# Six column tiles of the gated convolution computed as block products, and the skip term of the scan on ScalarE

## The chip, the cores and the metric

One NeuronCore of one Trainium2 chip runs the whole layer as a single program. The metric is device time in microseconds (us) of one execution. Executions of the kernel before took 2042.07, 2046.02 and 2046.38 us, median 2046.02 us.

## The reference

One layer of a hybrid decoder, 1024 positions by 1024 channels, all in float32. After a modulated RMS norm, one input projection makes five things: `z`, the `x/B/C` of a Mamba-2 scan, `dt`, the three inputs of a gated convolution, and two gates. What the change touches is this part:

```python
y_ssd = ssd_branch(z, xbc, dt_raw, ...)          # conv4 + silu, chunked scan, gate silu(z), grouped norm
#   in ssd_branch, after the scan:
y = y + d_skip[:, None] * xh                     # the skip term
y = y * silu(z); y = grouped_rmsnorm(y, norm_g, 4)
y_sc  = sc_b * causal_dwconv(sc_c * sc_h, conv_w)   # the gated convolution, 3 taps
mix   = (g_ssd * (y_ssd @ w_ssd_out) + g_sc * (y_sc @ w_sc_out)) @ w_o
```

The scan runs over 4 groups of 8 heads and, within a group, over 8 chunks of 128 positions with a state carried from chunk to chunk. The gated convolution has 1024 channels, so its three inputs are 24 column tiles of 128 channels. After the mixer comes a second half (norm, a gated MLP with convolution) that the change leaves alone.

## The kernel before, in words

Every float32 matrix is split into a rounded high part and a rest (line 130 on ScalarE, line 131 on VectorE), and a product is the sum of three products of such parts. A column tile of 128 channels by 1024 positions costs 48 matmuls of 128x512 this way (`gemm_into`, lines 147 to 156).

**Pair stage.** `Pair` (lines 178 to 276) computes two column tiles at once as a 2x2 block product with seven block multiplications instead of eight (the Strassen-Winograd scheme): 7 times 12 matmuls, 84 in place of 96. A loop over the string on line 621 computes 8 pairs of z, 8 pairs of gates and 12 pairs of x/B/C this way. Results go to DRAM.

**Scan.** Then come 32 chunks (`chunks`, line 807). Each chunk `n` is in three pieces: `ssd_front` loads `xb` and `zt` (for two chunks at once) and `E` (the cumulated decay, read with one row spread over all partitions), transposes `xb` (`xT`) and makes `xdt`, `sm`, `Bt`; `ssd_decay` makes on ScalarE `Cs` (an exponential), eight Relu operations on `E` and one exponential of it, and on VectorE the products with `xb` (line 717) and `sm` (line 727); `ssd_back` runs 16 pairs of small matmuls (`y`, line 737) that need `E`, `Cs` and the state of the chunk before, the matmul `st` of the new state, the norm of the two chunks before (matmuls into `half`), the skip term (line 765, four operations on VectorE that read `xb` and the finished `y`), the gate `zt` (line 767) and the square for the norm (line 769). `E`, `xb`, `zt` and `yo` have two buffers each, `xw` one and `state` two.

Between the pieces the loop on lines 810 to 817 puts pieces of the gated convolution. `sc_tile(i)` computes the three column tiles of 128 channels (`scc`, `sch`, `scb`) with plain `gemm`, in six steps of 24 matmuls; `STEPS` says how many steps follow each front: 0 to 2, 10 in a group of 8 chunks, 40 in all. The last 8 steps run after the scan. In this document these 128x512 matmuls between the chunks are called the column matmuls, and the matmuls of a chunk that start with `y` name the chunk: `y0_4` is group 0, chunk 4.

**Order.** The program is not run in the order written. A scheduler in the building library fixes the order on each engine before the run; calls inside `kept(...)` keep their place. On the chip every engine takes its list in that order and waits where an operand is missing. DMAs are issued by SyncE (SP), also in a fixed order.

After the scan `branches` multiplies the results by the output weights; it reloads `y_d` into tiles of the pool `qp` (`y_r`, line 845) and splits them.

```python
STEPS = (0, 1, 1, 2, 1, 2, 1, 2)
...
    if n + 1 < len(chunks):
        front = ssd_front(*chunks[n + 1])
    for _ in range(STEPS[n % 8]):
        next(proj, None)
    ssd_back(*this)
    if n + 1 < len(chunks):
        decay = ssd_decay(front)
```

Of the kernel before, what the change touches and what calls it, by code (L numbers as in the profile page):

```python
# [33 lines left out]
def hybrid_kernel(ctx: ExitStack, tc: tile.TileContext, x, pack, row_p, ada_w, w_in,  # L34
                  w_ssd, w_sc, w_o, w_up, w_down, out):
    nc = tc.nc
    V, S, G, PE, SY = nc.vector, nc.scalar, nc.gpsimd, nc.tensor, nc.sync
# [44 lines left out]
    def kept(ins):  # L82
        return tc.keep_in_program_order(ins)
# [4 lines left out]
    cv = {}  # L88
# [17 lines left out]
    ysc_d = [dram.tile([P, T], F32, name=f"ysc_d{i}") for i in range(KT)]  # L106
# [340 lines left out]
    def operands():  # L447
        return {n: [] for n in ("11", "12", "22", "s1", "s2", "s3", "s4")}
# [41 lines left out]
    A1 = operands()  # L490
# [121 lines left out]
    def gate_pair(g, j):  # L612
        us = Pair(A1, w_in[65 + j], w_in[66 + j], f"g{j}").finish()
        for o in range(2):
            S.activation(us[o], us[o], AF.Tanh, scale=0.5)
            SY.dma_start(gate_d[j + o], us[o])

    zs = [(z_pair, g, j) for g in range(NG) for j in (0, 2)]
    xs = [(xbc_pair, g, j) for g in range(NG) for j in (0, 2, 4)]
    gs = [(gate_pair, 0, 2 * n) for n in range(8)]  # L620
    for kind in "zzggggggggxxzxzxxzxxzxxzxxzx":
        fn, g, j = dict(z=zs, x=xs, g=gs)[kind].pop(0)
        fn(g, j)
# [18 lines left out]
    ld = ph.pool("ld", 2)  # L642
    sw = ph.pool("sw", 1)
# [5 lines left out]
    def bc(ap, n):  # L649
        return ap.unsqueeze(2).to_broadcast([P, ap.shape[1], n])  # L650
# [6 lines left out]
    def ssd_norm():  # L657
# [52 lines left out]
    def ssd_decay(front):  # L710
        nm, g, c, xb, zt, cs, hs, E, xdt, sm, Bt = front
        tS = tokS[:, c]
        Cs = cd = xw = None
        if c > 0:
            Cs = sw.tile([P, 8, P], F32, tag="Cs", name=f"Cs{nm}", bufs=2)
            S.activation(Cs, E, AF.Exp)  # L716
            V.tensor_tensor(Cs, Cs, xb[:, 5, cs].unsqueeze(1).to_broadcast([P, 8, P]), op=ALU.mult)
        if c < NCH - 1 and c > 0:
            cd = small.tile([P, 8], F32, tag="cd", name=f"cd{nm}")
            S.activation(cd, E[:, :, P - 1], AF.Exp)  # L720
        if c < NCH - 1:
            xw = sw.tile([P, 8, 64], F32, tag="xw", name=f"xw{nm}")
            G.tensor_tensor(xw, xdt, bc(tS[:, 3, hs], 64), op=ALU.mult)  # L723
        for h in range(8):
            S.activation(E[:, h, :], E[:, h, :], AF.Relu, scale=-1.0, bias=tS[:, 0, g * 8 + h:g * 8 + h + 1])  # L725
        S.activation(E, E, AF.Exp, scale=-1.0)  # L726
        V.tensor_tensor(E, E, sm.unsqueeze(1).to_broadcast([P, 8, P]), op=ALU.mult)  # L727
        return Cs, cd, xw

    def ssd_back(front, decay):  # L730
        nm, g, c, xb, zt, cs, hs, E, xdt, sm, Bt = front
        Cs, cd, xw = decay
        state = pairs.get("state")
        pt = bank(f"y{nm}")
        for j in range(4):
            def ymm(o, lhs, rhs, first, last):
                return PE.matmul(pt[o * 64:o * 64 + 64, j * P:j * P + P], lhs[:, 2 * j + o, :], rhs[:, 2 * j + o, :],  # L737
                                 start=first, stop=last)
            for o in range(2):
                ins = ymm(o, xdt, E, True, c == 0)  # L740
            if c > 0:
                for o in range(2):
                    ins = ymm(o, state, Cs, False, True)
        kept(ins)
        if c < NCH - 1:
            pst = bank(f"st{nm}")
            PE.matmul(pst, Bt, xw.rearrange("p h d -> p (h d)"), start=True, stop=True)  # L747
            pst = pst.rearrange("p (h d) -> p h d", h=8)
            ns = sw.tile([P, 8, 64], F32, tag="state", name=f"state{nm}", bufs=2)
            if c > 0:  # L750
                G.tensor_tensor(ns, state, bc(cd, 64), op=ALU.mult)
                V.tensor_tensor(ns, pst, ns, op=ALU.add)
            else:
                S.copy(ns, pst)
            pairs["state"] = ns
        if late:
            ssd_late()
        if pend:
            ssd_norm()
        if c % 2 == 0:  # L760
            pairs["out"] = ld.tile([P, 4, 256], F32, tag="yo", name=f"yo{nm}")
        yo = pairs["out"]
        y2 = yo[:, :, cs]
        for i in range(4):
            V.scalar_tensor_tensor(yo[:, i, cs], xb[:, i, cs], cv["ssd_d"][:, g * 4 + i:g * 4 + i + 1],  # L765
                                   pt[:, i * P:(i + 1) * P], op0=ALU.mult, op1=ALU.add)
        V.tensor_tensor(y2, y2, zt[:, :, cs], op=ALU.mult)
        sq = scratch.rearrange("p (a b) -> p a b", a=4)
        S.activation(sq, y2, AF.Square, scale=512 ** -0.5)
# [6 lines left out]
    def sc_tile(i):  # L776
        W = load_split(w_in[41 + i * 3], f"wsc{i}")
        pc = yield from gemm(A1p, W, f"scc{i}")
        ct = evt(f"sct{i}")
        S.copy(ct, pc)  # L780
        yield
        W = load_split(w_in[41 + i * 3 + 1], f"wsh{i}")
        ph = yield from gemm(A1p, W, f"sch{i}")
        V.tensor_tensor(ct, ph, ct, op=ALU.mult)
        w = cv["sc_w"][:, i * 3:i * 3 + 3]
        u = evt(f"scu{i}")
        S.activation(u, ct, AF.Copy, scale=w[:, 2:3])
        for k in (1, 0):
            s = 2 - k
            V.scalar_tensor_tensor(u[:, s:], ct[:, :T - s], w[:, k:k + 1], u[:, s:], op0=ALU.mult, op1=ALU.add)  # L790
        yield
        W = load_split(w_in[41 + i * 3 + 2], f"wsb{i}")
        pb = yield from gemm(A1p, W, f"scb{i}")
        V.tensor_tensor(u, pb, u, op=ALU.mult)
        if i < KT - 1:
            SY.dma_start(ysc_d[i], u)
        else:
            tail.append(u)
        yield

    def projections():
        for i in range(8):
# [514 lines left out]
```

## Time and profile before

| | |
|---|---|
| Median of three runs | 2046.02 us |
| The profiled execution, its own time | 2045.67 us |
| Span of its trace | 2044.0 us |
| Pair stage, scan, last 8 steps | 78 to 615, 615 to 985, 985 to 1012 us of the span |
| Output products of the branches, rest | 1012 to 1330, 1330 to 2044 us |

Busy time of TensorE is a sum of records that overlap, since matmuls are pipelined: a matmul of 128x512 has a record of 0.39 us. "Idle before" is the time in which an engine had no record, and the name behind the arrow is what ended it. The median lies 0.35 us above the profiled execution.

### The profile page before, as it was taken

To read this page: it belongs to the slowest core of one execution; us is meant where nothing else is said; L and a number is where in the kernel's file an instruction comes from. 1 tells how busy PE (TensorE), PEld (TensorE's weight loads), DVE (VectorE), ACT (ScalarE), POOL (GpSimd) and SP (SyncE) were. 2 spreads that over 40 slices of the span, in tenths; PEclk is the share of its full clock that TensorE was granted. 3 is DMA by queue.
4 is the path that set the end of the run, shared out by engine and by line. 5 is a ranking of instruction groups with operands and counts; after the bars stand their busy time and mean duration, and the time that the engine had idled before them with its cause. 6 is when DMAs were issued, how large, how long until landed. Compare 5 with 4: busy or idle time off the path is not lost. (4 is left out here: it accounts for less than half of the span.)

```text
span 2044.0 us, 25283 instructions
## 1 busy us (share of the span) xinstructions
PE 1993.1 (98%) x9476; PEld 1599.2 (78%) x9476; DVE 1453.3 (71%) x2016; ACT 978.8 (48%) x1572; POOL 152.0 (7%) x183
## 2 busy tenths in 40 slices
PE   7999999999999999999999999999999999989997
PEld 3788888888887777777887878876888888868886
DVE  4966567767768787786766555378887777767876
ACT  4665455544547656554422442246554454544443
POOL 1200000000002222121000010021000000000002
PEclk9999999999999999999999999999999999999999
DMA  8233223233245556553686567252222222268362
GB/s 298 77 125 120 104 98 120 100 111 120 99 139 208 167 186 206 170 165 127 203 275 230 196 228 266 93 187 71 103 72 93 83 73 93 83 228 282 119 232 98
DMA packets 128426, 308.97 MB, mean 151 GB/s; under 512 B 11184, under 2 KB 40240, under 8 KB 128304
## 3 DMA queue, kind: packets, MB, share of 16 engines
q1 hardware_dynamic: 128304, 307.36, 43.9%
q8 instruction: 74, 1.21, 0.2%
q14 instruction: 48, 0.39, 0.1%
HBM read 241.65 MB, written 65.67 MB: 150 GB/s over the span
## 5 line engine op out<-in xcount | busy, mean ns | idle before, releaser
L1042 DVE SCALAR_TENSOR_TENSOR uv<-u_u,pk,uv 128x1023 f32<-128x1023 f32 (+1 forms) x88 | 107.2, 1279 | 7.4 <-ACT uv L1039 7.4
L130 ACT CAST u_t_hi<-u_t 128x512 fp32r<-128x512 f32 x88 | 54.7, 623 | 119.8 <-PE u_p L172 108.6
L130 ACT CAST wy_hi<-wy_raw 128x1024 fp32r<-128x1024 f32 x32 | 33.6, 1051 | 133.4 <-PE bps L858 83.4
L594 DVE SCALAR_TENSOR_TENSOR xv<-x_u,pk,xv 128x1023 f32<-128x1023 f32 (+2 forms) x72 | 87.1, 1279 | 4.9 <-ACT xv L591 4.9
L725 ACT ACTIVATE E<-E,tokS 128x128 f32<-128x128 f32 x256 | 80.5, 390 | 14.5 <-DMA E<-acs_d 13.8
L130 ACT CAST u_hi<-u_raw 128x512 fp32r<-128x512 f32 x66 | 41.0, 622 | 73.2 <-PE u_p L172 73.2
L131 DVE TENSOR_TENSOR u_t_lo<-u_t,u_t_hi 128x512 fp32r<-128x512 f32 x88 | 60.2, 687 | 21.2 <-ACT u_t_hi L130 21.1
L716 ACT ACTIVATE Cs<-E 128x1024 f32<-128x1024 f32 x28 | 29.7, 1060 | 75.3 <-DMA E<-acs_d 75.2
L131 DVE TENSOR_TENSOR wy_lo<-wy_raw,wy_hi 128x1024 fp32r<-128x1024 f32 x32 | 39.1, 1221 | 37.4 <-ACT wy_hi L130 37.4
L130 ACT CAST x_t_hi<-x_t 128x512 fp32r<-128x512 f32 x48 | 29.9, 624 | 59.2 <-PE x_p L172 33.8
L1039 ACT ACTIVATE uv<-u_u,pk 128x1024 f32<-128x1024 f32 x44 | 52.5, 1238 | 2.3 <-DVE u_u L260 1.7
L737 PE MATMUL y<-E,xdt 128*64 128x128 f32 x512 | 51.1, 279 | 1.6 <-issue 1.6
L1189 POOL TENSOR_TENSOR dss<-dss,dss 128x1 f32<-128x1 f32 x8 | 3.8, 478 | 623.4 <-PE dx L1117 600.0
L130 ACT CAST x_hi<-x_raw 128x512 fp32r<-128x512 f32 x36 | 22.4, 623 | 53.2 <-PE x_p L172 25.2
L131 DVE TENSOR_TENSOR x_t_lo<-x_t,x_t_hi 128x512 fp32r<-128x512 f32 x48 | 32.5, 687 | 21.1 <-ACT x_t_hi L130 21.1
L727 DVE TENSOR_TENSOR E<-E,sm 128x1024 f32<-128x1024 f32 x32 | 41.1, 1286 | 8.5 <-ACT E L726 8.3
L131 DVE TENSOR_TENSOR u_lo<-u_raw,u_hi 128x512 fp32r<-128x512 f32 x66 | 45.0, 684 | 2.6 <-ACT u_hi L130 2.5
L256 DVE TENSOR_TENSOR u_u<-u_p,u_q 128x512 f32<-128x512 f32 x22 | 15.2, 691 | 44.3 <-PE u_p L173 44.3
L723 POOL TENSOR_TENSOR xw<-xdt,tokS 128x512 f32<-128x512 f32 x28 | 32.4, 1157 | 187.6 <-PE st L747 158.8
L765 DVE SCALAR_TENSOR_TENSOR yo<-xb,pk,y 128x128 f32<-128x128 f32 x128 | 39.3, 341 | 7.1 <-PE y L737 6.8
L737 PE MATMUL y<-Cs,state 128*64 128x128 f32 x448 | 43.9, 273 | 0.0
L896 DVE SCALAR_TENSOR_TENSOR gt<-gt,bps 128x512 f32<-128x512 f32 x32 | 20.5, 683 | 32.5 <-PE bps L859 30.2
(1865 smaller groups left out, 6716.2 us busy)
## 6 DMA issues: line engine op xcount, KB each, us to landing
u_raw<-in_w_up_dram SPq DMA_DIRECT2D x44, 512.0 KB, 3.5
E<-acs_d SPq DMA_DIRECT2D x32, 512.0 KB, 4.7
wy_raw<-in_w_ssd_dram SPq DMA_DIRECT2D x32, 512.0 KB, 4.9
x_raw<-in_w_in_dram SPq DMA_DIRECT2D x24, 512.0 KB, 3.4
xbc_d<-xv SPq DMA_DIRECT2D x24, 512.0 KB, 2.8
xb<-xbc_d SPq DMA_DIRECT2D x16, 768.0 KB, 6.3
f_d<-uv SPq DMA_DIRECT2D x22, 512.0 KB, 2.6
dm<-f_d SPq DMA_DIRECT2D x44, 256.0 KB, 6.0
```

What stands on the lines that cost most here:

```text
L130: S.copy(hi, src)
L131: V.tensor_sub(lo, src, hi.bitcast(F32))
L594: V.scalar_tensor_tensor(v[:, s:], u[:, :T - s], w[:, k:k + 1], v[:, s:], op0=ALU.mult, op1=ALU.add)
L716: S.activation(Cs, E, AF.Exp)
L723: G.tensor_tensor(xw, xdt, bc(tS[:, 3, hs], 64), op=ALU.mult)
L725: S.activation(E[:, h, :], E[:, h, :], AF.Relu, scale=-1.0, bias=tS[:, 0, g * 8 + h:g * 8 + h + 1])
L727: V.tensor_tensor(E, E, sm.unsqueeze(1).to_broadcast([P, 8, P]), op=ALU.mult)
L737: return PE.matmul(pt[o * 64:o * 64 + 64, j * P:j * P + P], lhs[:, 2 * j + o, :], rhs[:, 2 * j + o, :], start=first, stop=last)
L765: V.scalar_tensor_tensor(yo[:, i, cs], xb[:, i, cs], cv["ssd_d"][:, g * 4 + i:g * 4 + i + 1], pt[:, i * P:(i + 1) * P], op0=ALU.mult, op1= ...
L896: V.scalar_tensor_tensor(gts[o], gts[o], 1.0, ps[:, o, :], op0=ALU.add, op1=ALU.mult)
L1039: S.activation(v, us[j], AF.Identity, scale=w[:, 2:3], bias=cv["ffn_b"][:, t:t + 1])
L1042: V.scalar_tensor_tensor(v[:, s:], us[j][:, :T - s], w[:, k:k + 1], v[:, s:], op0=ALU.mult, op1=ALU.add)
```

## The change

Three parts. (1) The first two of the eight `sc_tile`s (`SCP = 2`, six of the 24 column tiles) leave the scan and become three pairs in the pair stage: `sch` and `scc` of tile 0, the same of tile 1, then `scb` of tiles 0 and 1 together, which reads the convolved values back from DRAM. The string of the pair stage gets three letters `s`, among the gates. `STEPS` sinks to 7 in a group, 28 in all. (2) The skip term: ScalarE multiplies `xb` by `ssd_d` into `yo` in `ssd_decay` of every second chunk (four operations of 128x256), and VectorE adds the finished `y` in one operation of 128x512. (3) `yo` gets three buffers; `xw` and `state` move into the rotating pool `qp` of ten tiles.

```diff
+SCP = 2
+    def sc_pair(b, i):
+        if not b:
+            ct, u = Pair(A1, w_in[41 + i * 3], w_in[42 + i * 3], f"sch{i}").finish()
+            V.tensor_tensor(ct, ct, u, op=ALU.mult)
+            sc_taps(i, ct, u)
+            SY.dma_start(ysc_d[i], u)
+            return
+        us = Pair(A1, w_in[43 + i * 3], w_in[46 + i * 3], f"scb{i}").finish()
+        for o in range(2):
+            u = evt(f"scu{i + o}")
+            SY.dma_start(u, ysc_d[i + o])
+            V.tensor_tensor(us[o], us[o], u, op=ALU.mult)
+            SY.dma_start(ysc_d[i + o], us[o])
...
-    for kind in "zzggggggggxxzxzxxzxxzxxzxxzx":
+    for kind in "zzgggsggsggsgxxzxzxxzxxzxxzxxzx":
...
+        if c % 2 == 0:
+            yo = ld.tile([P, 4, 256], F32, tag="yo", name=f"yo{nm}", bufs=3)
+            for i in range(4):
+                S.activation(yo[:, i, :], xb[:, i, :], AF.Copy, scale=cv["ssd_d"][:, g * 4 + i:g * 4 + i + 1])
+            pairs["yo"] = yo
...
-            xw = sw.tile([P, 8, 64], F32, tag="xw", name=f"xw{nm}")
+            xw = qt(f"xw{nm}").rearrange("p (h d) -> p h d", h=8)
...
-            ns = sw.tile([P, 8, 64], F32, tag="state", name=f"state{nm}", bufs=2)
+            ns = qt(f"state{nm}").rearrange("p (h d) -> p h d", h=8)
...
-        for i in range(4):
-            V.scalar_tensor_tensor(yo[:, i, cs], xb[:, i, cs], cv["ssd_d"][:, g * 4 + i:g * 4 + i + 1],
-                                   pt[:, i * P:(i + 1) * P], op0=ALU.mult, op1=ALU.add)
+        V.tensor_tensor(y2, pt.rearrange("p (i l) -> p i l", i=4), y2, op=ALU.add)
...
-        for i in range(8):
+        for i in range(SCP, KT):
             yield from sc_tile(i)
...
-    STEPS = (0, 1, 1, 2, 1, 2, 1, 2)
+    STEPS = (0, 1, 1, 1, 1, 1, 1, 1)
```

The scheduler's order changes with it. On TensorE, in group 0, between the new state `st0_4` of chunk 4 and the `y` of chunk 5, before (12 column matmuls of `scb0` and `scc1` stand there):

```order
L747 MATMUL st0_4_5445<-xw0_4_5370,Bt0_4_5263 128x512
L670 MATMUL half_4958<-rs0_2_5355,ones_82 128x128
L695 MATMUL xT0_6_5491<-ident_77,xb0_6_5485 128x128 x4
L156 MATMUL scb0_5403<-h12_6h_681,wsb0_lo_5400 128x512
L156 MATMUL scb0_5403<-h22_6h_523,wsb0_lo_5400 128x512
L153 MATMUL scb0_5403<-h12_7h_699,wsb0_hi_5399 128x512
L154 MATMUL scb0_5403<-h12_7l_700,wsb0_hi_5399 128x512
L153 MATMUL scb0_5403<-h22_7h_542,wsb0_hi_5399 128x512
L660 MATMUL half_4958<-ones_82,scratch_170 128x1
```

The same place in the changed program, to the end of `y0_5`'s first pairs:

```order
L775 MATMUL st0_4_5850<-xw0_4_5777,Bt0_4_5697 128x512
L693 MATMUL half_5393<-rs0_2_5760,ones_82 128x128
L718 MATMUL xT0_6_5892<-ident_77,xb0_6_5886 128x128 x4
L683 MATMUL half_5393<-ones_82,scratch_170 128x1
L722 MATMUL half_5393<-xb0_6_5886 128x128
L724 MATMUL half_5393<-ident_77,xb0_6_5886 128x128
L765 MATMUL y0_5_5936<-E0_5_5789,xdt0_5_5796 64x128 x2
```

No column matmul stands between chunks 4 and 5 any more; 20 of `scb2` follow right behind `y0_5` instead. Between chunks 2 and 3 there are 5 (15 before), between 3 and 4 there are 4 (33 before).

On ScalarE, in group 0, the operations on chunk 5's `E` and what follows them in the changed program (`scratch` from `yo0_4` is the square of chunk 4; `yo0_6` are the new products with `ssd_d`):

```order
L744 ACTIVATE Cs0_5_5869<-E0_5_5789 128x1024
L748 ACTIVATE cd0_5_5872<-E0_5_5789 128x8
L753 ACTIVATE E0_5_5789<-E0_5_5789,tokS_180 128x128 x5
L730 COPY Bt0_5_5802<-half_5393 128x128
L753 ACTIVATE E0_5_5789<-E0_5_5789,tokS_180 128x128 x3
L740 ACTIVATE yo0_6_5973<-xb0_6_5886,pk_75 128x256
L754 ACTIVATE E0_5_5789<-E0_5_5789 128x1024
L740 ACTIVATE yo0_6_5973<-xb0_6_5886,pk_75 128x256 x3
L744 ACTIVATE Cs0_6_5978<-E0_6_5890 128x1024
L748 ACTIVATE cd0_6_5981<-E0_6_5890 128x8
L753 ACTIVATE E0_6_5890<-E0_6_5890,tokS_180 128x128
L792 ACTIVATE scratch_170<-yo0_4_5767 128x512
```

The square of chunk 4 stands behind three operations that read chunk 6's `E`. On VectorE, in the same place, the last rows ahead of the product that completes chunk 5's `E`:

```order
L780 TENSOR_TENSOR state0_4_5852<-st0_4_5850,state0_4_5852 128x512
L694 TENSOR_TENSOR yo0_2_5564<-yo0_2_5564,half_5393 128x4x128
L790 TENSOR_TENSOR yo0_4_5767<-yo0_4_5767,zt0_4_5682 128x4x128
L685 TENSOR_SCALAR ym0_3_5858<-half_5393 128x1
L745 TENSOR_TENSOR Cs0_5_5869<-Cs0_5_5869,xb0_4_5680 128x1024
L688 TENSOR_SCALAR rs0_3_5862<-ident_77,yr0_3_5860 128x128
L793 TENSOR_TENSOR scratch_170<-scratch_170 128x256
L755 TENSOR_TENSOR E0_5_5789<-E0_5_5789,sm0_5_5800 128x1024
```

The sum over the square of chunk 4 (`scratch`, 128x256) now stands ahead of chunk 5's `E`; before, the sum ahead of `E0_5` was that of chunk 3, and chunk 4's came later. Chunk 5's `E` so stands behind an operation on chunk 6's; in no other chunk of the changed program does a chunk's `E` stand behind the next one's in this way.

## Rows read from the trace of the kernel before

**Rows 1.** The page: busy time of the engines, and TensorE's granted clock in 40 slices.
```profile
PE 1993.1 (98%) x9476; PEld 1599.2 (78%) x9476; DVE 1453.3 (71%) x2016; ACT 978.8 (48%) x1572; POOL 152.0 (7%) x183
...
PEclk9999999999999999999999999999999999999999
```

**Rows 2.** Windows: stretch, length, busy us (instructions) of five engines, clock, DMA share, GB/s.
```profile
78.00:615.00 537.00, 535.63 (x2349) 437.19 (x2348) 364.04 (x501) 277.50 (x415) 0.90 (x2) 1.00 0.31 111
615.00:985.00 370.00, 363.23 (x2374) 287.06 (x2372) 285.08 (x524) 210.53 (x449) 83.14 (x84) 1.00 0.53 173
```

**Rows 3.** Timeline of TensorE: first and last of 12 column matmuls in a row.
```profile
609.91 0.39 PE L153 MATMUL scc<-h_1h,wsc_hi 128*128 128x512 f32 x1
...
612.40 0.39 PE L156 MATMUL scc<-a21b_2h,wsc_lo 128*128 128x512 f32 x1
```

**Rows 4.** Tile g_p, the eight gate pairs: durations, then first and last start.
```profile
L171 PE MATMUL g_p<-h_0h,g_hi x8: 389/389/476, 107.3 to 242.8; 128*128 128x512 f32 x8
```

**Rows 5.** Tile x_p: the first and the last x pair, 17 pairs apart.
```profile
L171 PE MATMUL x_p<-h_0h,x_hi x12: 389/389/389, 262.0 to 588.5; 128*128 128x512 f32 x12
```

**Rows 6.** Waits of TensorE in the scan, 615 to 985 us: total, times, longest.
```profile
PE xT L695 <- DMA xb<-xbc_d: 3.0, 6, 0.9
PE y L737 <- issue: 1.6, 2, 0.8
PE half L660 <- DVE yo L671: 1.4, 3, 0.9
```

**Rows 7.** Timeline of TensorE, scan of group 0: start, length, then idle before.
```profile
632.13 0.44 PE L737 MATMUL y<-E,xdt 128*64 128x128 f32 x4 [0.83 <-issue]
...
639.61 0.44 PE L737 MATMUL y<-E,xdt 128*64 128x128 f32 x4 [0.74 <-issue]
...
643.38 0.63 PE L695 MATMUL xT<-ident,xb 128*128 128x128 f32 x4 [0.53 <-DMA xb<-xbc_d]
...
660.10 0.44 PE L737 MATMUL y<-E,xdt 128*64 128x128 f32 x4
...
662.00 1.12 PE L747 MATMUL st<-xw,Bt 128*128 128x512 f32 x2
...
667.04 0.44 PE L737 MATMUL y<-E,xdt 128*64 128x128 f32 x4
```

**Rows 8.** VectorE in the scan by line and form: count, busy us, mean ns, idle before.
```profile
L727 DVE TENSOR_TENSOR E<-E,sm 128x1024 f32<-128x1024 f32 x32 | 41.1, 1286 | 8.5 <-ACT E L726 8.3
L765 DVE SCALAR_TENSOR_TENSOR yo<-xb,pk,y 128x128 f32<-128x128 f32 x128 | 39.3, 341 | 7.1 <-PE y L737 6.8
...
L752 DVE TENSOR_TENSOR state<-st,state 128x512 f32<-128x512 f32 x24 | 16.5, 689 | 2.1 <-PE st L747 1.8
L770 DVE TENSOR_TENSOR scratch<-scratch 128x256 f32<-128x256 f32 x32 | 15.1, 472 | 9.6 <-ACT scratch L769 9.5
```

**Rows 9.** Timeline of ScalarE in the scan: start, length, operation.
```profile
645.65 1.05 ACT L130 CAST wsc_hi<-wsc_raw 128x1024 fp32r<-128x1024 f32 x1 [0.99 <-PE sch L154]
...
650.91 1.14 ACT L787 ACTIVATE scu<-sct,pk 128x1024 f32<-128x1024 f32 x1
...
653.69 1.06 ACT L716 ACTIVATE Cs<-E 128x1024 f32<-128x1024 f32 x1 [0.70 <-DMA E<-acs_d]
654.66 0.20 ACT L720 ACTIVATE cd<-E 128x8 f32<-128x8 f32 x1
654.89 2.46 ACT L725 ACTIVATE E<-E,tokS 128x128 f32<-128x128 f32 x8
657.37 1.06 ACT L726 ACTIVATE E<-E 128x1024 f32<-128x1024 f32 x1
658.51 0.63 ACT L769 ACTIVATE scratch<-yo 128x512 f32<-128x512 f32 x1
```

**Rows 10.** Tile E in the scan: a Relu on one head, and its loads.
```profile
L725 ACT ACTIVATE E<-E,tokS x256: 384/388/412, 617.2 to 949.4; 128x128 f32<-128x128 f32 x128
...
DMA to landing us min/median/max: 3.3/4.5/7.8
```

More of the change, by code (lines that the diff above doesn't have):

```diff
@@ L616, in gate_pair, with sc_taps @@
             SY.dma_start(gate_d[j + o], us[o])
+    def sc_taps(i, ct, u):
+        w = cv["sc_w"][:, i * 3:i * 3 + 3]
+        S.activation(u, ct, AF.Copy, scale=w[:, 2:3])
+        for k in (1, 0):
+            s = 2 - k
+            V.scalar_tensor_tensor(u[:, s:], ct[:, :T - s], w[:, k:k + 1], u[:, s:], op0=ALU.mult, op1=ALU.add)
+    def sc_pair(b, i):
[11 more added lines that the diff above has]
+            SY.dma_start(ysc_d[i + o], us[o])
+    scs = [(sc_pair, b, i) for i0 in range(0, SCP, 2) for b, i in ((0, i0), (0, i0 + 1), (1, i0))]
     zs = [(z_pair, g, j) for g in range(NG) for j in (0, 2)]
@@ L620, in hybrid_kernel @@
     gs = [(gate_pair, 0, 2 * n) for n in range(8)]
-    for kind in "zzggggggggxxzxzxxzxxzxxzxxzx":
-        fn, g, j = dict(z=zs, x=xs, g=gs)[kind].pop(0)
+    for kind in "zzgggsggsggsgxxzxzxxzxxzxxzxxzx":
+        fn, g, j = dict(z=zs, x=xs, g=gs, s=scs)[kind].pop(0)
         fn(g, j)
@@ L727, in ssd_decay @@
         V.tensor_tensor(E, E, sm.unsqueeze(1).to_broadcast([P, 8, P]), op=ALU.mult)
-        return Cs, cd, xw
+        return Cs, cd, xw, pairs["yo"]
     def ssd_back(front, decay):
         nm, g, c, xb, zt, cs, hs, E, xdt, sm, Bt = front
-        Cs, cd, xw = decay
+        Cs, cd, xw, yo = decay
         state = pairs.get("state")
@@ L759, in ssd_back @@
             ssd_norm()
-        if c % 2 == 0:
-            pairs["out"] = ld.tile([P, 4, 256], F32, tag="yo", name=f"yo{nm}")
-        yo = pairs["out"]
         y2 = yo[:, :, cs]
-        for i in range(4):
-            V.scalar_tensor_tensor(yo[:, i, cs], xb[:, i, cs], cv["ssd_d"][:, g * 4 + i:g * 4 + i + 1],
-                                   pt[:, i * P:(i + 1) * P], op0=ALU.mult, op1=ALU.add)
+        V.tensor_tensor(y2, pt.rearrange("p (i l) -> p i l", i=4), y2, op=ALU.add)
         V.tensor_tensor(y2, y2, zt[:, :, cs], op=ALU.mult)
@@ L784, in sc_tile @@
         V.tensor_tensor(ct, ph, ct, op=ALU.mult)
-        w = cv["sc_w"][:, i * 3:i * 3 + 3]
         u = evt(f"scu{i}")
[L787 to L790, printed above, removed]
+        sc_taps(i, ct, u)
         yield
```

## The prediction

> **What bounds the kernel now.** I read the page's busy line first, then the windows by stage, then the waits of TensorE in the scan, and last its timeline there. TensorE is the busiest engine, and its clock is at the upper of its two levels, 2.4 GHz, in every slice [rows 1]. That busy time is a sum of overlapping records, so the windows have to show that it leaves no gaps: in the pair stage TensorE lacks 1.4 us of 537, in the scan 6.8 us of 370 [rows 2]. Both stages are therefore bound by what TensorE is given to do. In the scan, the gaps are short waits for `xb`, for `y`'s operands and for the norm [rows 6]. VectorE is busy for 77% of the scan, ScalarE for 57% [rows 2]: neither is full, but each chunk is a chain through both, and the column matmuls are what covers that chain. So two things decide: how many matmuls TensorE has, and whether the chain stays covered once column matmuls are taken out of the scan.
>
> **Column tiles as pairs.** Twelve column matmuls run from 609.91 to 612.40, 11 steps, so one costs 0.226 us of TensorE's time [rows 3]; the record of 0.39 us overlaps its neighbours and is not the price. Six tiles of 48 leave the scan: 288 x 0.226 = 65.2 us. Three pairs come into the pair stage. Eight gate pairs start 7 pairs apart over 135.5 us, 19.4 us each [rows 4]; the x and z pairs take 326.5 us for 17, 19.2 us each [rows 5]. Three cost 57.6 to 58.1 us, taken as 57.9. **Net -7.3 us**, between -7.1 and -7.6.
>
> What the new pairs give other engines (the splits, two or three products and taps of 1.2 to 1.3 us, a reload of 512 KB twice) lies beside a stage in which VectorE is busy 68%, ScalarE 52% and the DMAs 31% [rows 2]. The two reloads stand on SP's queue between the two weight loads of the pair after next, which are needed some 19 us later; if that cover failed, each would cost one landing, some 4 us. I take 0.
>
> **Skip term.** VectorE loses 4 operations of 0.34 us in each chunk and gets one of 128x512 that reads PSUM, 0.69 us by the state's add of that shape: 0.7 us less in each chunk [rows 8]. ScalarE gets two operations of 128x256 in each chunk. No row has that shape; it lies between the Relu on 128x128, 0.39 us [rows 10], and the square on 128x512, 0.63 us [rows 9], and I take 0.47. That is 0.9 us more in each chunk. Where 24 column matmuls stand between two chunks TensorE needs 4.2 + 24 x 0.226 = 9.7 us for a chunk (the 4.2: from `y0_4` to `y0_5` 6.94 us pass with 12 column matmuls, no gap on the way [rows 7]). ScalarE needs for one about 1.0 + 0.2 + 2.5 + 1.0 + 0.6 [rows 9] + 0.9, some 6.2 us, and about 1 for a column step. Covered, 0 us.
>
> The Trainium skill, "ScalarE: Activation LUTs", section "Rules for kernel authors", says that a multiplication belongs on VectorE, not ScalarE. It speaks against this part; the sum here stays as it is as long as TensorE sets the pace of a chunk. What it would do otherwise is the last rival.
>
> **Buffers.** `xb` was last read by the skip term behind `y`; now it is free as soon as `Cs` is multiplied, about a chunk earlier, and its next load moves ahead on SP's queue. The 3.0 us that TensorE waits for `xb` [rows 6] should go, 0.5 of which lies in the stretch treated next [rows 7]: -2.5. In exchange the heads of groups 2 and 3 have 27 column matmuls up to their second `y` where 30 and 34 stood; 3 x 0.226 = 0.7 us less cover for the first, with at most that as a stall: +0.5. **-2.0 us**, between -4 and +2. With `xw` and `state` in `qp`, the reloads of `y_d` can no longer come in mid-scan; they are issued near its end, still ahead of 8 steps x 24 x 0.226 = 43 us of column work. I take 0; without that cover they would cost one load, some 5 us.
>
> **The uncovered stretch.** The order shows the price of the scheduler's choice: between the `y` of chunks 2, 3, 4 and 5 of group 0 stand 5, 4 and 0 column matmuls. TensorE's own work there is 5.3, 5.1 and 4.2 us. Three waits follow.
> - Ahead of `y0_3` the first `scb2` needs a cast that ScalarE does behind chunk 3's exponential. I estimate 0.9 us.
> - From the exponential of `E0_3` to that of `E0_4` ScalarE has two casts, a square, `Cs`, `cd`, eight Relu, the product `scu2` and the exponential: 2.0 + 0.6 + 1.0 + 0.2 + 2.5 + 1.1 + 1.0 = 8.4 us [rows 9]. With the 0.9 already lost 7.5 remain against 5.1: 2.4 us.
> - Chunk 5's `E` waits on VectorE behind the sum over chunk 4's square; that square stands on ScalarE behind three operations on chunk 6's `E`; and that `E` can only be loaded when `y0_4` has released the buffer. From the end of `y0_4`: load 4.5 [rows 10], `Cs` 1.0, `cd` 0.2, one Relu 0.3, square 0.6 [rows 9], sum 0.4, product 1.2 [rows 8] = 8.2 us. TensorE has 4.2 - 1.9 = 2.3 us of its own there (`y` itself lasts 1.9, 660.10 to 662.00 [rows 7]): 5.9 us. With a load of 3.3 or 7.8 us [rows 10] it is 4.7 or 9.2.
>
> Together 9.2 us. Before, the same stretch lost 0.83 + 0.74 + 0.53 = 2.1 [rows 7]. **+7.1 us**, between +3 and +12. The column matmuls displaced from here follow behind `y0_5`, where nothing lacked cover, so they don't earn it back.
>
> **Sum.** -7.3 - 2.0 + 7.1 = -2.2 us. The profiled execution took 2045.67 us, 0.35 below the median; the forecast is 2043.5 us.
>
> **Rivals.**
> *The stretch keeps the old pace (faster).* In the kernel before, chunks follow each other in 6.94 us (`y0_4` to `y0_5`) and 7.48 us with a gap of 0.74 (`y0_1` to `y0_2`) [rows 7]. At 7.0 us the three gaps are 1.7, 1.9 and 2.8, 6.4 in all, +4.3 over before. If moreover the later waits nearly vanish (6.8 - 2.1 = 4.7 us now, of which 4.2 go), the sum is -7.3 + 4.3 - 4.2 = -7.2: 2038.5 us. For it: VectorE has less to do in each chunk. Against it: the order on VectorE ties chunk 5 to chunk 6's load, which no chunk after the first group's had to wait for so directly.
>
> *The loads of `E` set the pace (slower).* They land in 3.3 to 7.8 us [rows 10]. In the covered scan a late one costs ScalarE idle time only. In the stretch two of them, `E0_4` and `E0_6`, lie on the chain, and at the two heads with 27 column matmuls one each. At 7 us instead of 4.5 that is 2 x 2.5 + 2 x 2.0 = +9.0 over the forecast: 2052.5 us. It decides from a landing of about 5.5 us on. For it: the chunks come faster, so the DMAs, 53% busy in the scan, have less time between loads. Against it: the median is 4.5, and the weights of six tiles are no longer loaded in the scan.
>
> *ScalarE sets the pace (slower).* If the products with `ssd_d` lie in front of exponentials that are waited for, each gap with few column matmuls grows by two of them, 0.94 us; some eight gaps in the changed order hold 17 or fewer: +7.5 over the forecast, 2051.0 us. That is where the rule of "ScalarE: Activation LUTs" would lead. By the rows ScalarE was idle 43% of the scan and waited for loads, which speaks against it.
>
> **How the numbers follow.** 0.2%, 4.1 us, is about what a measurement of this kernel can tell from no change: faster means below 2041.9, slower above 2050.1. Forecast 0.50, old pace 0.33, loads 0.12, ScalarE 0.05. The forecast's own range is 2040 to 2048; a small part of it counts as faster. So faster 0.37, same 0.48, slower 0.15. The range 2037.5 to 2051.0 takes in the old pace and the lower end of the slower cases, and leaves out about 2 in 10.
>
> **What would show it.** Right: the pair stage longer by about 58 us without gaps on TensorE; no wait of `xT` for `xb`; in group 0 gaps ahead of `y0_4` and `y0_5` that come to 7 to 10 us, the second the longer; later chunks nearly without gaps. Wrong: gaps there under 6 us (old pace), many waits for `E` on TensorE in groups 1 to 3 (loads), or gaps between the three new pairs and their neighbours.

## The result, and the profile after

The changed kernel took 2058.85 us (median of four runs, 2056.77 to 2060.37), the kernel before 2046.20 us beside it. The ratio is 1.0063, with a 95% interval of 1.0044 to 1.0082: some 13 us slower. Forecast were 2043.5 us, between 2037.5 and 2051.0: the result lies outside the range, and the time moved the other way. The profiled execution of the changed kernel took 2056.77 us with a span of 2055.0.

The windows of the changed kernel, in the columns of [rows 2]: the pair stage, the scan, and two pieces of 12 us out of group 0.

```profile
78.00:672.00 594.00, 592.88 (x2603) 484.60 (x2602) 401.36 (x552) 299.48 (x452) 0.89 (x2) 1.00 0.31 111
672.00:985.00 313.00, 294.57 (x2032) 226.63 (x2032) 267.21 (x404) 219.13 (x494) 85.62 (x83) 0.98 0.56 186
713.00:725.00 12.00, 7.25 (x45) 5.38 (x45) 10.70 (x17) 9.17 (x24) 3.69 (x4) 0.65 0.31 95
725.00:737.00 12.00, 10.71 (x63) 8.98 (x64) 10.31 (x13) 5.48 (x15) 3.44 (x2) 0.78 0.63 198
```

Against [rows 2], the pair stage is as full as before; the loss lies in the scan. There TensorE lacks 18.4 us of 313 where it lacked 6.8 of 370, VectorE is 85% busy where it was 77%, and in 24 us of it the mean granted clock is under 1.00. From the end of the last x pair to the first output product 359.2 us pass, against 404.2 before: 45.0 us fewer, where the 288 column matmuls taken out were worth 65.2. So the scan lost 20.2 us. The pairs themselves add 57.1 us. Behind the first output product the two kernels run alike, to about 1 us.

TensorE's waits in the scan of the changed kernel (672 to 985 us), as [rows 6]:

```profile
PE y L765 <- issue: 9.0, 9, 2.8
PE half L683 <- DVE yo L694: 4.8, 9, 1.2
PE half L722 <- DVE ym L685: 1.6, 2, 0.8
```

The 3.0 us of `xT` for `xb` [rows 6] are gone from the list, as forecast. Longer waits for `y`'s operands (9.0 us, 1.6 before) and for `yo` (4.8 us, 1.4 before) are there instead. TensorE's timeline in the stretch of group 0 with few column matmuls, as [rows 7]. `y0_1` starts at 688.20, `y0_2` at 698.61, `y0_4` at 714.71, `y0_5` at 726.29 and `y0_6` at 742.71:

```profile
688.20 0.44 PE L765 MATMUL y<-E,xdt 128*64 128x128 f32 x4 [0.50 <-issue]
...
698.61 0.44 PE L765 MATMUL y<-E,xdt 128*64 128x128 f32 x4 [1.48 <-issue]
...
699.07 0.42 PE L765 MATMUL y<-E,xdt 128*64 128x128 f32 x4
...
700.50 1.13 PE L775 MATMUL st<-xw,Bt 128*128 128x512 f32 x2
...
711.67 0.49 PE L722 MATMUL half<-xb 128*128 128x128 f32 x2 [0.82 <-DVE ym L685]
...
714.71 0.70 PE L765 MATMUL y<-E,xdt 128*64 128x128 f32 x4 [2.44 <-issue]
...
715.59 0.67 PE L765 MATMUL y<-E,xdt 128*64 128x128 f32 x4
...
718.32 2.00 PE L775 MATMUL st<-xw,Bt 128*128 128x512 f32 x2
...
721.70 0.38 PE L683 MATMUL half<-ones,scratch 128*128 128x1 f32 x2 [0.72 <-DVE yo L694]
722.91 0.49 PE L722 MATMUL half<-xb 128*128 128x128 f32 x2 [0.83 <-DVE ym L685]
...
726.29 0.69 PE L765 MATMUL y<-E,xdt 128*64 128x128 f32 x4 [2.78 <-issue]
...
729.90 1.34 PE L775 MATMUL st<-xw,Bt 128*128 128x512 f32 x2
...
742.71 0.44 PE L765 MATMUL y<-E,xdt 128*64 128x128 f32 x4
```

And `y0_6` of the kernel before, whose `y0_1` starts at 632.13 [rows 7]:

```profile
682.13 0.44 PE L737 MATMUL y<-E,xdt 128*64 128x128 f32 x4
```

From `y0_1` to `y0_6` the kernel before took 50.0 us with 119 column matmuls, the changed kernel 54.5 us with 74. With 0.226 us taken off for each column matmul, the changed kernel is 14.7 us longer there. The gaps are those of the forecast: 0.82 + 2.44 us between `y0_3` and `y0_4`, 0.72 + 0.83 + 2.78 us between `y0_4` and `y0_5`.

What the forecast did not have is the clock. From the first four matmuls with `E` to the next four (four with `Cs` stand between them) 0.46 us pass at 698.61 and 0.88 at 714.71: `y` and `st` run there at 1.2 instead of 2.4 GHz. Before it fell, TensorE had done four column matmuls behind `y0_3` and waited 0.82 and 2.44 us with three small matmuls between. The rows give the price: from the start of `y` to `st` it is 1.89 us for `y0_2`, 3.61 for `y0_4` and 3.61 for `y0_5`, and `st0_4` takes 2.00 us instead of 1.13. That is some 4.3 us of TensorE's time. The windows at 0.65 and 0.78 lose more clock, about 12 x 0.35 + 12 x 0.22 = 6.8 us, but part of it while TensorE waited.

The second thing shows on VectorE. The rows are its operations in the scan by line and form; the mean in ns stands after the busy time. First the kernel before, then the changed kernel (one of its 32 `rs` lies behind 985 us):

```profile
L767 DVE TENSOR_TENSOR yo<-yo,zt 128x512 f32<-128x512 f32 x32 | 22.7, 709 | 0.0
...
L665 DVE TENSOR_SCALAR rs<-ident,yr 128x128 f32<-128x128 f32 x32 | 9.2, 286 | 14.0 <-POOL yr L121 13.9
```

```profile
L790 DVE TENSOR_TENSOR yo<-yo,zt 128x512 f32<-128x512 f32 x32 | 29.6, 925 | 0.2
L789 DVE TENSOR_TENSOR yo<-y,yo 128x512 f32<-128x512 f32 x32 | 21.9, 684 | 10.5 <-PE y L765 8.9 <-DMA wsb_raw<-in_w_in_dram 1.6
...
L688 DVE TENSOR_SCALAR rs<-ident,yr 128x128 f32<-128x128 f32 x31 | 20.8, 672 | 9.5 <-POOL yr L122 7.3
```

The new addition costs 21.9 us where the old skip term cost 39.3 [rows 8], as forecast. But `rs` (line 688, the norm's scale times the identity) and the product with `zt` (line 790), which the change doesn't touch, grew by 11.6 and 6.9 us: the saving of 17.4 is spent. The timeline of both engines in the changed kernel says on what:

```profile
801.12 1.04 POOL L779 TENSOR_TENSOR state<-state,cd 128x512 f32<-128x512 f32 x1 [4.43 <-DVE state L780]
801.49 1.22 DVE L790 TENSOR_TENSOR yo<-yo,zt 128x512 f32<-128x512 f32 x1
...
802.70 0.68 DVE L720 TENSOR_TENSOR xdt<-xT,tokS 128x512 f32<-128x512 f32 x1
...
802.92 0.55 POOL L122 TENSOR_TENSOR yr<-ym,nhalf 128x1 f32<-128x1 f32 x1 [0.76 <-DVE ym L685]
...
803.50 1.15 DVE L688 TENSOR_SCALAR rs<-ident,yr 128x128 f32<-128x128 f32 x1
803.52 1.04 POOL L751 TENSOR_TENSOR xw<-xdt,tokS 128x512 f32<-128x512 f32 x1
...
804.57 0.28 DVE L726 TENSOR_TENSOR sm<-half,mask 128x128 f32<-128x128 f32 x1
```

`rs` ends within 0.1 us of GpSimd's `xw`, and the product with `zt` ends some 0.5 us after GpSimd's `state`. In the scan of the changed kernel 14 of 32 `rs` lie beside an `xw`: 1.14 us in the mean, the other 18 take 0.29. Of the products with `zt`, 19 lie beside a `state` (1.09 us; the others 0.69). `xdt` and the new addition, which read PSUM, take 0.68 beside `xw` or `state` or not. In the kernel before no `rs` and two products with `zt` met GpSimd. The same two engines there:

```profile
764.63 1.05 POOL L723 TENSOR_TENSOR xw<-xdt,tokS 128x512 f32<-128x512 f32 x1 [11.78 <-PE st L747]
...
765.19 0.68 DVE L671 TENSOR_TENSOR yo<-yo,half 128x512 f32<-128x512 f32 x1
...
765.63 1.05 POOL L751 TENSOR_TENSOR state<-state,cd 128x512 f32<-128x512 f32 x1
...
765.78 0.34 DVE L765 SCALAR_TENSOR_TENSOR yo<-xb,pk,y 128x128 f32<-128x128 f32 x1
...
766.04 0.68 DVE L697 TENSOR_TENSOR xdt<-xT,tokS 128x512 f32<-128x512 f32 x1
...
766.71 0.68 DVE L767 TENSOR_TENSOR yo<-yo,zt 128x512 f32<-128x512 f32 x1
766.87 0.93 POOL L121 TENSOR_TENSOR yr<-ym,nhalf 128x1 f32<-128x1 f32 x1 [0.19 <-DVE ym L662]
...
767.84 0.29 DVE L665 TENSOR_SCALAR rs<-ident,yr 128x128 f32<-128x128 f32 x1 [0.45 <-POOL yr L121]
```

There `xw` waited 11.78 us for `st`, the last reader of its one tile, so `xw` and `state` ran behind `st`, beside VectorE's operations that read PSUM, the last of the skip term among them. With the rotating pool, `xw` runs as soon as `xdt` is there, behind `yr`, just when VectorE wants `rs`.

The Trainium skill, "SBUF — State Buffer", section "Who interferes with whom", says that VectorE and GpSimd share a pair of ports, held for a whole instruction by the one that issues first, and that VectorE wants it with two inputs in SBUF or in its two-port modes. The trace agrees: 0.29 against 1.14 us for `rs`, 0.69 against 1.09 for the product with `zt`, no difference for the operations that read PSUM. That `rs` is in such a mode no row shows, and which of `rs` and `xw` issued first their records, 0.02 us apart, don't tell.

### The profile page after: what moved, and what is told of

Read it like the earlier page. It is cut to its first block, busy times and chain, and to the rows that moved or that the text cites. A ratio compares the mean times of both kernels' runs of the same rounds, so it can differ in the third digit from the quotient of the medians.

```text
span 2055.0 us, 25330 instructions
## 1 busy us (share of the span) xinstructions
PE 1990.6 (97%) x9440; PEld 1592.4 (77%) x9440; DVE 1479.4 (72%) x1956; ACT 1014.2 (49%) x1661; POOL 155.5 (8%) x183
## 5 line engine op out<-in xcount | busy, mean ns | idle before, releaser
L765 PEld LDWEIGHTS y<-E,xdt 128*64 128x64 f32 x512 | 33.6, 142 | 20.3 <-issue 15.5
```

## The experiments

There are three theories. **Stretch** ("cover" in the first expectations): the uncovered stretch in group 0 costs gaps and clock. **GpSimd**: VectorE's operations that read SBUF alone last longer beside GpSimd's `xw` and `state`. **Rivals**: the skip term or the pairs cost time by themselves, VectorE's count of operations decides ("count"), or the loads of `E` do. A chunk with 24 column matmuls or fewer is called thin. Each ratio is to the kernel before, executed beside that run; its medians there lie between 2044.08 and 2045.89 us, so where the medians of two groups of runs are compared, 2 us mean little. An experiment called covered has a list of 32 numbers in `STEPS`, one for each chunk, with `STEPS[n]` in the loop. That of run 1, with 31 steps:

```diff
-    STEPS = (0, 1, 1, 1, 1, 1, 1, 1)
+    STEPS = (2, 1, 1, 1, 1, 1, 1, 1, 0, 1, 1, 1, 1, 1, 1, 2, 0, 1, 1, 1, 1, 1, 1, 1, 0, 1, 1, 1, 1, 1, 1, 1)
```

**1. Other steps (above), nothing else.**

> The changed kernel with another list of steps: 2 before chunk 0's y, a second one at the end of group 1, the rest as changed. By the order every chunk but the last of a group then has 15 or more column matmuls behind its y; the arithmetic is the same. Theory 'cover' (the stretch with 5, 4 and 0 column matmuls costs both the gaps and the fall of TensorE's clock): both go, 10 to 16 us less than the changed kernel, 2043 to 2049 us, clock 1.00 throughout the scan. Rival 'skip term' (ScalarE's extra products and the moved buffers slow each chunk): 2055 us or more. Rival 'pairs' (the pair stage costs more than it saves): 2055 us or more.

2051.86 us, ratio 1.0031 (1.0019 to 1.0043), between the forecasts: "cover" allowed at most 2049, and a clock of 1.00 where one window (732 to 744 us) still has 0.86. Covering the stretch is worth about 7 us of 13 by the medians, 6.5 by the ratios, but the kernel stays slower than before. Chunks with 24 column matmuls take 10.4 us in the mean, not the 9.7 that TensorE needs; `rs` is as long as in the changed kernel (below).

**2. Parts 2 and 3 alone** (`SCP = 0`, old string, old steps).

> Parts 2 and 3 of the change alone (skip term on ScalarE, three yo, xw and state in the rotating pool); no pairs, the old steps. Its order has 5 and 4 column matmuls behind the y of chunks 2 and 3 of group 0, but 64 behind chunk 4. 'Cover': part of the loss, without the stretch at chunk 5: 2046 to 2053 us, with a clock under 1.00 in at most one 12 us window. 'Skip term': all of the loss and the pairs' gain taken away, 2060 to 2068 us. 'Pairs': 2044 to 2047 us.

2058.13 us, 1.0062 (1.0050 to 1.0074): more than "cover" allowed, less than "skip term". Both miss.

**3. Part 1 alone** (old skip term and buffers).

> Part 1 of the change alone (three pairs, 7 steps in a group), with the old skip term and buffers. Its order has 0 and 4 column matmuls behind the y of chunks 5 and 6 of group 0 and 8 at one place each in groups 2 and 3. 'Cover': the pairs' -7.3 and a stretch of its own of +5 to +14: 2044 to 2053 us. 'Skip term': the gain of the pairs alone, 2037 to 2041 us. 'Pairs': 2055 us or more.

2060.95 us, 1.0074 (1.0062 to 1.0086), above all forecasts but that of "pairs", which runs 4 and 12 rule out. Each half of the change is as slow as the whole; the costs don't add.

**4. The kernel before with 7 steps in a group instead of 10, nothing else.**

> The kernel before with 7 steps in a group instead of 10 and nothing else: the same column matmuls, 12 more steps of them after the scan, and the same order inside the scan as in part 1 alone. 'Cover': 2051 to 2061 us, that is part 1 alone plus 7 to 8. 'Skip term' and 'pairs': no change against the kernel before, 2044 to 2048 us.

2072.77 us, 1.0125 (1.0110 to 1.0140). Thinning the cover costs 28 us without any of the change's parts, 12 more than "cover" allowed. Run 3 has the same steps and the pairs as well, and takes 11.8 us less: the pairs do save time. 8.1 us are told by the stages above, the rest is not placed.

**5. 32 steps, one more than in run 1 (the 33 below is a miscount); the base of the next three.**

```diff
+    STEPS = (2, 2, 1, 1, 1, 1, 1, 1, 0, 2, 1, 1, 1, 1, 1, 1, 0, 1, 1, 1, 1, 1, 1, 1, 0, 1, 1, 1, 1, 1, 1, 1)
```

> The changed kernel with 33 steps in the scan, two more than the covered kernel, and a list under which every chunk but a group's last has 15 or more column matmuls behind its y. It is the base of the next three. With thicker cover at group 1's head 0 to 3 us less than the covered kernel: 2048 to 2053 us.

2057.85 us, 1.0063 (1.0051 to 1.0075): 5 us above the forecast. The time from the x pairs to the first output product is 3.7 us shorter than in run 1, but 14 us into the output products stands this line of TensorE's timeline:

```profile
1025.99 0.79 PE L878 MATMUL bps<-y_8h,wy_lo 128*128 128x512 f32 x1 [8.06 <-DVE wy_lo L132]
```

With 96 column matmuls behind the last chunk the output products start before VectorE has made their operands, and in the 12 us from 1024 the granted clock is 0.68. With 120 (run 1) that wait is 1.35 us, with 144 (run 10) no wait there reaches 1 us. So the base carries a cost of its own behind the scan.

**6. The addition as four operations.**

```diff
-        V.tensor_tensor(y2, pt.rearrange("p (i l) -> p i l", i=4), y2, op=ALU.add)
+        for i in range(4):
+            V.tensor_tensor(yo[:, i, cs], pt[:, i * P:(i + 1) * P], yo[:, i, cs], op=ALU.add)
```

> The base, with the one addition of the finished y (128x512) written as four of 128x128, the form the old skip term had on VectorE, so that 0.7 us of VectorE's time come back in each chunk; ScalarE's products stay. Theory 'GpSimd' (the operations of VectorE that read SBUF alone last longer whenever GpSimd's products of state or xw run; the old skip term, which reads PSUM, lay in that time and the shorter one no longer does): rs falls from 0.7 to 0.3-0.4 us, yo times zt from 0.9 to 0.70-0.78, and the kernel takes 4 us less up to 4 us more than the base. Theory 'count' (VectorE's time by number and length of operations decides): rs and zt stay, +8 to +17 us.

2053.91 us, 1.0045 (1.0032 to 1.0058): more work for VectorE, and by the medians 4 us less than the base (the intervals just overlap). VectorE's `zt` and `rs` of run 6:

```profile
L791 DVE TENSOR_TENSOR yo<-yo,zt 128x512 f32<-128x512 f32 x32 | 27.0, 842 | 0.1
...
L688 DVE TENSOR_SCALAR rs<-ident,yr 128x128 f32<-128x128 f32 x31 | 11.4, 369 | 13.3 <-POOL yr L122 12.9
```

`rs` fell from 0.66 to 0.37 us in the mean of all 32, `zt` only from 0.95 to 0.84, less than forecast. "Count", which wanted 8 us more, falls.

**7. `rs` on GpSimd.**

```diff
-        V.tensor_scalar(rs, ident, r, None, op0=ALU.mult)
+        G.tensor_scalar(rs, ident, r, None, op0=ALU.mult)
```

> The base, with rs (128x128, identity times the norm's scale) made by GpSimd itself behind yr. VectorE loses an operation that takes 0.7 us in the base. 'GpSimd': VectorE's busy time in the scan falls by 15 to 22 us, chunks with 24 columns go from 10.4 toward 9.8 us, the kernel takes 4 to 12 us less than the base. 'Count': by its undisturbed 0.29 us only 9 us less on VectorE, 0 to 4 us less in all. A third way, that ScalarE's loads of E set the pace: no change.

2047.79 us, 1.0009 (1.0001 to 1.0018): 10 us under the base by the medians. Up to the first output product it is 8 us shorter than the base; the rest comes behind it. Chunks with 24 column matmuls take 9.9 us in the mean, 10.2 in the base.

**8. `state` times `cd` on VectorE.**

```diff
-                G.tensor_tensor(ns, state, bc(cd, 64), op=ALU.mult)
+                V.tensor_tensor(ns, state, bc(cd, 64), op=ALU.mult)
```

> The base, with the product of state and cd (128x512) made by VectorE instead of GpSimd: 24 more operations of about 0.7 us on VectorE, and GpSimd left with xw and yr. 'GpSimd': rs and yo times zt fall to 0.3 and 0.7 us, which pays for the new operation: within 5 us of the base. 'Count': +10 to +17 us.

2051.78 us, 1.0031 (1.0019 to 1.0043), 6 us under the base, with 24 more operations on VectorE: "count" falls again, and "GpSimd" had allowed 5. Its product with `zt`:

```profile
L790 DVE TENSOR_TENSOR yo<-yo,zt 128x512 f32<-128x512 f32 x32 | 21.9, 683 | 0.1
```

So `state` is what made `zt` long. `rs` stays at 0.58, beside `xw`, where 0.3 was expected.

**9. The changed kernel and its own steps, with `rs` on GpSimd. 10. The same with 30 steps** (2 ahead of chunk 0 and 1 behind each later front in group 0, the changed kernel's list in the others).

> The changed kernel with its own steps, and only rs made by GpSimd: the stretch with 5, 4 and 0 column matmuls stays in the order. 'GpSimd' and 'stretch' as two separate costs: the scan's later chunks come closer to 9.8 us, the stretch and its clock stay: 3 to 9 us less than the changed kernel, 2049 to 2055 us. If the stretch is the whole loss: no change, 2056 to 2060 us.

> Both cures: rs on GpSimd, and 30 steps in the scan that cover group 0, with 144 column matmuls left behind the last chunk (the 96 of the 33-step kernels left the branches waiting 7 to 8 us for their weights' rests). If the two costs add up: 2038 to 2044 us, the first kernel here below the kernel before. If the steps only move a wait: 2046 us or more.

2054.14 us, 1.0043 (1.0030 to 1.0055), and 2041.54 us, 0.9978 (0.9969 to 0.9987). Run 9 is 4.7 us under the changed kernel by the medians, with intervals that overlap; run 10 is another 12.6 below. Both lie where two separate costs would put them, but separate they are not. `y0_1` and `y0_6` in run 9:

```profile
689.05 0.44 PE L765 MATMUL y<-E,xdt 128*64 128x128 f32 x4 [0.46 <-issue]
...
738.80 0.44 PE L765 MATMUL y<-E,xdt 128*64 128x128 f32 x4
```

With the same 74 column matmuls it is 49.75 us where the changed kernel took 54.51: 4.8 us less, as much as run 9 saves in all. Its gaps from `y0_1` to `y0_5` come to 6.1 us (10.6 in the changed kernel), and the granted clock falls for half as long (0.86 in each of two windows, 701 to 713 and 713 to 725). So a part of the stretch's loss was the longer `rs`, and what one cure is worth depends on the other. Covering saves 12.6 us with `rs` on GpSimd (9 against 10), and about 7 with `rs` on VectorE (run 1). Scan of run 10, to be read against the changed kernel's second line at the top:

```profile
672.00:985.00 313.00, 304.38 (x2106) 235.71 (x2107) 257.80 (x380) 220.36 (x499) 116.61 (x116) 1.00 0.57 192
```

**11. Parts 2 and 3 alone, covered** (`2, 1, 1, 2, 1, 2, 1, 2`, then the old list). **12. Part 1 alone, covered** (31 steps).

> Parts 2 and 3 alone (10 steps in a group, no pairs), with two steps ahead of chunk 0 so that no stretch is left uncovered. 'Stretch': the skip part is harmless under thick cover, VectorE's longer operations included: 2041 to 2047 us, 11 to 16 us under the same without the cover. 'GpSimd' as a cost in covered chunks too: 2050 us or more.

> Part 1 alone with the old skip term, covered as in the kernel above (31 steps in the scan). VectorE has 0.7 us more by count in each chunk than in the covered kernel with the whole change, but rs and zt undisturbed. 'GpSimd': as long as the covered kernel with the whole change, 2047 to 2055 us, chunks of 24 columns at 9.7 to 10.5 us. 'Count': 2058 us or more.

2047.59 us, 1.0013 (1.0004 to 1.0021), and 2045.33 us, 0.9999 (0.9990 to 1.0008). Covering takes 10.5 us off run 2 and 15.6 off run 3. Run 11 falls between its two forecasts, run 12 below both. Part 1 with the old skip term is 6.5 us better than the whole change at the same number of steps (run 1). VectorE in run 12, the old skip term, `zt`, `rs`:

```profile
L788 DVE SCALAR_TENSOR_TENSOR yo<-xb,pk,y 128x128 f32<-128x128 f32 x128 | 40.0, 341 | 5.3 <-PE y L760 5.1
...
L790 DVE TENSOR_TENSOR yo<-yo,zt 128x512 f32<-128x512 f32 x32 | 22.7, 708 | 0.0
...
L688 DVE TENSOR_SCALAR rs<-ident,yr 128x128 f32<-128x128 f32 x32 | 9.2, 287 | 12.7 <-POOL yr L122 12.6
```

**13. Run 12 with `rs` on GpSimd. 14. The kernel before with `rs` on GpSimd.**

> Part 1 alone, covered (the same steps as e12), old skip term, and rs made by GpSimd. If VectorE's time by the chunk sets the pace of thin chunks: VectorE loses 0.29 us and the wait for yr in each chunk, 3 to 8 us less than e12, 2037 to 2042 us, level with the whole change cured the same way. If the loads of E set it: no change, 2043 to 2047 us.

> The kernel before with rs made by GpSimd and nothing else. Chunks there have 36 column matmuls on average and TensorE sets the pace: 2043 to 2047 us, no gain that can be measured. If VectorE's time is worth something there too: 2036 to 2042 us.

2042.01 us, 0.9985 (0.9975 to 0.9996), and 2047.95 us, 1.0017 (1.0006 to 1.0029). Run 13 is 3.3 us under run 12 by the medians, with intervals that overlap. With the 30 column matmuls that a chunk of the kernel before has in the mean (10 steps of 24 for 8 chunks; the 36 above is a slip) `rs` on GpSimd gains nothing and costs a little.

**15. Run 10 with three buffers of `E`.**

```diff
-        rs = sw.tile([P, P], F32, tag="rs", name=f"rs{nm}")
+        rs = qt(f"rs{nm}")[:, 0:P]
-        E = ld.tile([P, 8, P], F32, tag="E", name=f"E{nm}")
+        E = ld.tile([P, 8, P], F32, tag="E", name=f"E{nm}", bufs=3)
```

> The covered kernel with rs on GpSimd (e10), and three buffers for E instead of two (rs moves into the rotating pool to make room). If the loads of E set the pace of thin chunks: ScalarE's waits for E (about 30 us) mostly go and the kernel takes 4 to 10 us less, 2032 to 2038 us. If VectorE does: within 3 us of e10, 2039 to 2045 us.

2044.60 us, 0.9996 (0.9986 to 1.0006). ScalarE waited 20.6 us for `E` ahead of `Cs` in run 10; it is not among the longest seven of run 15, where `Cs` waits 20.6 us for `y` instead. There is no gain, so the loads of `E` don't set the pace.

**16. Run 10 with part 3 undone. 17. Run 1 with `xw` alone undone. 18. Run 1 with part 3 undone.** The line of run 17, and the three of 16 and 18:

```diff
-            xw = qt(f"xw{nm}").rearrange("p (h d) -> p h d", h=8)
+            xw = sw.tile([P, 8, 64], F32, tag="xw", name=f"xw{nm}")
...
-            ns = qt(f"state{nm}").rearrange("p (h d) -> p h d", h=8)
+            ns = sw.tile([P, 8, 64], F32, tag="state", name=f"state{nm}", bufs=2)
...
-            yo = ld.tile([P, 4, 256], F32, tag="yo", name=f"yo{nm}", bufs=3)
+            yo = ld.tile([P, 4, 256], F32, tag="yo", name=f"yo{nm}")
```

> The covered kernel with rs on GpSimd (e10), and part 3 undone: two buffers of yo, xw and state in their own one and two tiles. By the forecast's term the buffers are worth 2 us, by its bounds -2 to +4: 2040 to 2046 us. If xw with a single buffer holds GpSimd and through it the new state: 2046 us or more.

> The covered kernel e1_covered with the same steps and one line undone: xw in its own single tile, as in the kernel before; state and yo stay as changed. If xw's place in the rotating pool brings it beside rs: rs back to 0.29-0.35 us (0.73 in e1_covered), VectorE 10 to 14 us less busy in the scan, and 3 to 9 us less than e1_covered, 2043 to 2049 us. If rs is long for another reason: no change, 2050 to 2054 us.

> The covered kernel e1_covered with the same steps and all of part 3 undone, rs on VectorE. By the forecast's term for the buffers it would be 2 us longer than e1_covered, by that term's bounds 4 us shorter to 2 longer... taken together 2048 to 2056 us. If xw beside rs is what part 3 costs: rs at 0.29-0.35 us and 4 to 11 us less than e1_covered, 2041 to 2048 us; yo times zt stays above 0.8 us, since the shortened addition is kept.

2039.53 us, 0.9970 (0.9959 to 0.9980), the lowest median of all, though its interval overlaps with run 10's; 2046.45 us, 1.0008 (0.9999 to 1.0016); 2047.69 us, 1.0013 (1.0004 to 1.0021). Run 17 differs from run 1 in that one line, and each chunk has the same number of column matmuls behind its `y`. `rs` on VectorE and `xw` on GpSimd, run 1, then run 17:

```profile
L688 DVE TENSOR_SCALAR rs<-ident,yr 128x128 f32<-128x128 f32 x30 | 22.2, 740 | 8.5 <-POOL yr L122 6.3
...
L751 POOL TENSOR_TENSOR xw<-xdt,tokS 128x512 f32<-128x512 f32 x28 | 31.4, 1124 | 21.0 <-DVE xdt L720 20.1
```

```profile
L688 DVE TENSOR_SCALAR rs<-ident,yr 128x128 f32<-128x128 f32 x32 | 9.2, 287 | 8.5 <-POOL yr L122 7.3
...
L751 POOL TENSOR_TENSOR xw<-xdt,tokS 128x512 f32<-128x512 f32 x28 | 35.3, 1260 | 131.6 <-PE st L775 118.3 <-DVE xdt L720 10.2 <-DVE Cs L745 2.8
```

Now `xw` waits 118.3 us for `st` again, and `rs` takes 0.287 us each time. So 13 us of VectorE, and 5.4 us of the kernel by the medians (4.7 by the ratios, whose intervals lie apart), hung on where one tile of GpSimd lies. All of part 3 undone (18) is worth no more than that line.

## Why the prediction was wrong

**Column tiles as pairs, -7.3: held.** 57.1 us for three pairs (57.9 forecast), 65.2 taken out, no gaps in the pair stage: -8.1.

**The uncovered stretch, +7.1: the place was right, the size was not.** It came to +14.7 (from `y0_1` to `y0_6`). The gaps were forecast well. Ahead of `y0_4` TensorE is idle for 3.3 us (2.4 forecast), ahead of `y0_5` for 4.3 (5.9 forecast), and the chain from the end of `y0_4` (718.32) to `y0_5` (726.29) took 8.0 us where 8.2 were forecast. All gaps from `y0_1` to `y0_5` are 10.6 us against 2.1 before: +8.5. The term that the forecast put at nothing is the clock, which fell to 1.2 GHz over `y0_4` and `y0_5`: some 4.3 us. The remaining 2 us are not placed. And the forecast took VectorE's operations at the durations of the kernel before: with `rs` out of GpSimd's way (run 9) the stretch is 4.8 us shorter.

**Buffers, -2.0, between -4 and +2: the sign was wrong.** The wait for `xb` went as forecast. But "`xw` and `state` in `qp`" was costed for reloads only, and what GpSimd would then run beside was put at nothing. The single tile of `xw` had been a wait that kept GpSimd in step with `st`, and nothing queued behind it lacked time. Free of it, `xw` runs beside `rs`, which takes 11.6 us longer in the scan of the changed kernel. In the covered kernel the one line costs about 5 us (1 against 17).

**Skip term, "Covered, 0 us": undersized in thin chunks.** The forecast set ScalarE's 6.2 us against TensorE's 9.7 and took VectorE's as falling by 0.7 a chunk. VectorE's time did not fall, since the shorter addition leaves the product with `zt` beside `state` (0.93 us instead of 0.71) and `rs` beside `xw`. VectorE is busy for 85% of the scan, and a chunk with 24 column matmuls takes about 10.2 us in the mean instead of 9.7. With part 3 undone the skip term shows no gain (18 against 12, both with 31 steps, one of them at another place): 1.0013 against 0.9999.

**Rivals and signs.** The old pace did not come: `y0_4` to `y0_5` took 11.6 us, not 7.0. The loads of `E` fall by run 15, and ScalarE's idle time for them had already shrunk. ScalarE as the bound is not borne out by any row, though no run takes its products alone away. None of the three had VectorE and GpSimd in it. Most signs named for a right forecast came: the longer pair stage without gaps, no wait of `xT`, 7.6 us of gaps ahead of `y0_4` and `y0_5`, the second the longer. They asked for gaps alone, and neither for the clock nor for VectorE's durations. Only "later chunks nearly without gaps" failed: of 18.4 us idle in the scan 10.6 lie in the stretch.

Taken together, by the traces of the two kernels: -8.1 for the pairs, +14.7 from `y0_1` to `y0_6`, and +6.0 for the chunks from there to the last one, counted in the same way. That is +12.6; the profiled executions differ by 11.1, the medians by 12.65. How the +14.7 and the +6.0 divide between the stretch and GpSimd is open in part, since each cure changes what the other is worth. That both are causes the runs show: 9 against 10 for the cover, 1 against 17 for `xw` beside `rs`.

## What to carry over

A wait that costs nothing can hold two engines apart: before giving a tile another buffer, look what its writer will then run beside, and read VectorE's mean durations with GpSimd's timeline next to them. When matmuls leave a loop, count for every chunk what is left of them between the waits (order, not average), and cost a row of gaps with TensorE's clock in it. The change pays once both are seen to: covered steps, `rs` on GpSimd and the old buffers give 2039.53 us, 0.9970 of the kernel before. What the skip term adds to that is not shown: the pairs without it, cured in the same two ways, give 0.9985 (run 13), and the intervals overlap.

## What the runs showed that was not expected

GpSimd loses as well, where VectorE starts first: in the changed kernel `yr` takes 0.55 us at 802.92, beside `xdt`, which reads PSUM. The one behind a product with `E` that started just before takes 1.39, and so do four others that stand like it (1.39 to 1.40 us).

```profile
812.84 1.21 DVE L755 TENSOR_TENSOR E<-E,sm 128x1024 f32<-128x1024 f32 x1
...
813.06 1.39 POOL L122 TENSOR_TENSOR yr<-ym,nhalf 128x1 f32<-128x1 f32 x1 [0.76 <-DVE ym L685]
```

And more work on VectorE was no slower twice: four additions for one (run 6) and a product brought to the busier engine (run 8), both under the base by the medians.
